# A two-layer encoder step on one core: the first feature pair of SwiGLU in plain products for all chunks, cC's down product in one pass over eight banks, norm sums in two rows

## Chip, cores and metric

The kernel runs on one core of one Trainium2 chip. The metric is the device time of one execution in microseconds. In the kernel before, every product on TensorE (PE) is of 128x128 weights with 128x384 activations in fp32r.

## What is computed

Two encoder layers over a prompt of 1024 frames and eight samples of 16 frames. The part that the change touches is the same in both layers:

```python
def _rms(x, g):
    y = x * lax.rsqrt(jnp.mean(x * x, axis=-1, keepdims=True) + EPS)
    return y * g

def _swiglu(a, w_gate, w_up, w_down):
    return (jax.nn.silu(a @ w_gate) * (a @ w_up)) @ w_down

for i in range(2):                      # layers; D_MODEL = 1024, D_FF = 2816
    a = _rms(h, norm_mix_pre[i])
    mix = ...                           # attention and its out-projection
    h = h + _rms(mix, norm_mix_post[i])
    f = _swiglu(_rms(h, norm_ffn_pre[i]), ffn_w_gate[i], ffn_w_up[i], ffn_w_down[i])
    h = h + _rms(f, norm_ffn_post[i])
    gate = jax.nn.sigmoid(_rms(h, ple_norm[i]) @ ple_w_gate[i] + ple_b_gate[i])
    h = h + gate * (p[i] @ ple_w_proj[i])
```

## The kernel before

The 1024 + 128 frames are 1152 columns, in three **chunks** of 384. `layer_tail` (from L1066) does everything of a layer behind the attention; its argument `order` names the chunks cC, cA, cB in the order in which the out-projection finishes them. Features lie along the partitions, so a 1024-wide vector of a chunk is eight rows of 128x384.

**Products.** fp32 accuracy is had from two fp32r parts: an operand is rounded (a cast on ACT, `round_r`, L139) and the rest is kept as its low part (a subtraction on DVE, `low_part`, L145). `mm3` (L215 to L217) then makes three matmuls for one product: high by high, weight high by activation low, weight low by activation high. Products gather in two kinds of PSUM banks: six in pool `psmm` (tag "mm") and two in `psst` (tag "st"); the norms use the latter.

**SwiGLU.** The 22 blocks of 128 hidden features are taken as 11 **pairs** g, each with a gate and an up **matrix** (g, up) of two blocks A and B. Chunk cC gets plain products (`plain`, 24 matmuls for a block). Chunks cA and cB go together through a form of Strassen with seven products instead of eight (`product`, 12 matmuls each, banks X, Y, Z): weights A, B and their combinations C, D (sums on DVE by `s_sum`, L1315), by activations Y11, Y21 (the halves of cA), Y22 (a half of cB) and T1 to T4, differences of rows of cA and cB (`minus`, L1229). `operand` splits each into parts. A bank is copied out (`copied`, ACT at L1353 or DVE at L1355), added to (`added`, L1359) and finished by silu or by the product with silu (`final`, `direct`); `diff` makes combinations of the results, and `store` sends rows to DRAM: `hc_d` for cC (22 rows), `t_d` for the seven combinations of cA and cB.

Pair 0 (`EARLY`) is split in time: cC's products of both matrices come first, and the seven products of each after them, in the order

```python
product("X", "A", 0, "Y11", new=True)
product("Z", "A", 1, "Y21", new=True, frees=[wa])
product("X", "C", 1, "T2")
product("Y", "D", 0, "T3", new=True)
product("X", "C", 0, "T1", frees=[wc])
product("X", "D", 1, "Y22", frees=[wd])
product("Y", "B", 1, "T4", frees=[wb])
```

**Down product.** `kstep` (from L1513) loads one row of hidden features, splits it, splits one 128x512 half of a block of `w_down`, and makes four output blocks' products (12 matmuls). cC takes two passes of 22 such steps over four "mm" banks, one for each half of the outputs, so each row of `hc_d` is loaded and split twice. The weights are loaded in halves of 256 KB (`wd_load`, L1506). Seven Strassen passes of 11 steps for cA and cB follow.

**Norms.** `plan_rms` squares a chunk on ACT (L360, four squares of 128x768). The first goes into `acc` (one buffer), DVE adds the other three to it (L365) and folds its two rows (L367); PE sums over the partitions (`total`, tile pstat, L233), DVE takes the root in twelve small operations (L241 to L247), PE spreads it over the partitions (`spread`, tile prms, L254) and ACT copies it to `rr` (L380). After the out-projection each chunk has two norms: one of the output, followed by scaling and the residual sum (L424, L428), and one ahead of SwiGLU, followed by scaling (L1195). After the down product there are two again.

**What sets the order.** `Plan` is a list scheduler that runs when the program is built: every step has an engine, a cost in microseconds, steps it comes after, due times and counts of buffers that it takes and frees. It writes out the order of PE, ACT and DVE; SP issues all DMAs in the plan's order too. At run time each engine follows its order and waits on semaphores.

Of the kernel before, what the change touches and what calls it, by code (L numbers as in the profile page):

```python
# [10 lines left out]
F32 = mybir.dt.float32  # L11
F32R = mybir.dt.float32r
# [6 lines left out]
P = 128  # L19
D = 1024  # L20
KT = 8
# [67 lines left out]
def tile_kernel(ctx: ExitStack, tc: tile.TileContext, i, o, upto=99):  # L89
# [260 lines left out]
    def plan_rms(plan, src, after, out="rr", slot=None, ready=()):  # L350
# [4 lines left out]
        def square(k):  # L355
            if k:
                box[k] = t = tp.tile([P, 2, C], F32, name="sq", tag="sq", bufs=NSQ)
            else:
                box["acc"] = t = tp.tile([P, 2, C], F32, name="acc", tag="acc", bufs=1)
            nc.scalar.activation(t, src()[:, 2 * k:2 * k + 2, :], AF.Square)  # L360

        def gather(k):
            acc = box["acc"]
            if k < 4:
                nc.vector.tensor_tensor(acc, acc, box.pop(k), ADD)  # L365
            else:
                nc.vector.tensor_tensor(acc[:, 0], acc[:, 0], acc[:, 1], ADD)  # L367

        def sums():
            box["ps"] = total(box["acc"][:, 0])  # L370
# [11 lines left out]
        last = begin = plan.add(ACT, 0.735, step(square, 0), after[0], takes=["acc"])  # L382
        for k in range(1, 4):
            box["read"] = s = plan.add(ACT, 0.735, step(square, k), after[k] + [begin], takes=["sq"])
            last = plan.add(DVE, 0.87, step(gather, k), [s, last], frees=["sq"])
        last = plan.add(DVE, 0.47, step(gather, 4), [last])
# [679 lines left out]
    def layer_tail(l, oc, Wo, oa0, order, specs_kv=(), more=None):  # L1066
# [18 lines left out]
        plan = Plan(act=4 + (len(oa0[1]) == KT), raw=1, w0=2, w1=3, acc=1, sq=NSQ, rr=NRR, st=2, mm=6, hs=STB, row=NROW, y=2)  # L1085
# [163 lines left out]
        operand("Y21", cA, 4)  # L1249
        operand("Y22", cB, 4)  # L1250
# [39 lines left out]
        def matrix(g, up, when=1):  # L1290
# [58 lines left out]
            def copied(n, bank, eng=ACT):  # L1349

                def fn():
                    if eng == ACT:
                        nc.scalar.copy(put_row(temp(n)), ps(bank))  # L1353
                    else:
                        nc.vector.tensor_copy(put_row(temp(n)), ps(bank))  # L1355
                add(eng, 0.37 if eng == ACT else 0.47, fn, r=[(m, "ps", bank)], w=[(g, temp(n))], takes=["row"], **soon())
# [31 lines left out]
            whole = ("A", x1, [(m, "x", 0)]), ("B", x2, [(m, "x", 1)])  # L1388
            early = m in EARLY
            if when == 0:  # L1390

                loads()
                tags[m] = [parts_of(m, *x) for x in whole]
                unload()
# [4 lines left out]
            loads()  # L1399
            wa = tags[m][0] if early else parts_of(m, *whole[0])  # L1400
            add(DVE, 0.6, step(s_sum, 1), r=[(m, "x", 1)], w=[(m, "s1")], takes=["y"])
            add(DVE, 0.6, step(s_sum, 2), r=[(m, "x", 0), (m, "s1")], w=[(m, "s2")])
            wc = parts_of(m, "C", lambda: sums[m][:, 0], [(m, "s1"), (m, "s2")])
            add(DVE, 0.6, step(s_sum, 3), r=[(m, "x", 0), (m, "x", 1), (m, "s1")], w=[(m, "s3")])
            add(DVE, 0.6, step(s_sum, 4), r=[(m, "x", 0), (m, "s2")], w=[(m, "s4")])
            wd = parts_of(m, "D", lambda: sums[m][:, 1], [(m, "s3"), (m, "s4")])
            release(["y"], [(m, f"s{n}") for n in range(1, 5)])
            wb = tags[m][1] if early else parts_of(m, *whole[1])
            unload()

            product("X", "A", 0, "Y11", new=True)
            copied("11", "X")
            if not early:
                plain(0, "A", [])
                plain_out(0)
            product("Z", "A", 1, "Y21", new=True, frees=[wa])
            added("11", "Z", ["mm"])
            final("11")
            product("X", "C", 1, "T2")
            copied("21", "X", DVE if up else ACT)  # L1420
            product("Y", "D", 0, "T3", new=True)
            product("X", "C", 0, "T1", frees=[wc])
            copied("22", "X")
            added("22", "Y", [])
            final("22")
            if not early:
                plain(1, "B", [])
                plain_out(1)
            product("X", "D", 1, "Y22", frees=[wd])
            direct("r12", lambda: ps("X"), (m, "ps", "X"))  # L1430
            product("Y", "B", 1, "T4", frees=[wb])
            added("21", "Y", ["mm"])
            final("21")
            marks.append(plan.tiles[-1])
            if up:
# [12 lines left out]
        tags = {}  # L1448
        EARLY = (0, 0), (0, 1)
        for m in EARLY:  # L1450
            matrix(*m, when=0)
        for g in range(FFT // 2):
            for up in range(2):
                matrix(g, up)
# [48 lines left out]
        def wd_load(f, half):  # L1503
            if half == 0 and f % 3 == 0:
                wds[f // 3] = ap_.tile([P, 3, 1024], F32, name="wd", tag="act")
# [741 lines left out]
```

## Time and profile before

| | us |
|---|---|
| median of 3 runs (lowest to highest) | 2988.94 (2987.65 to 2989.17) |
| the profiled execution's own time | 2988.7 |
| its span in the profile | 2986.9 |

The span is what the profile covers; times in its rows count from its start. Layer 0's out-projection ends at 715.6 us, its down product begins at 1277.8; in layer 1 it is 2054.8 and 2605.9. A row of the timeline has the start, the length, engine, line, operation, written and read tiles with their shapes, and in brackets how long the engine was idle before it and who released it. A row of a stage table has the stage, its length, the busy time of PE, of its weight loads, of DVE, ACT and POOL (with counts), PE's granted clock as a share of full speed, the busy share of the DMA engines and GB/s.

### The profile page before, as it was taken

To read this page: it belongs to the slowest core of one execution; us is meant where nothing else is said; L and a number is where in the kernel's file an instruction comes from. 1 tells how busy PE (TensorE), PEld (TensorE's weight loads), DVE (VectorE), ACT (ScalarE), POOL (GpSimd) and SP (SyncE) were. 2 spreads that over 40 slices of the span, in tenths; PEclk is the share of its full clock that TensorE was granted. 3 is DMA by queue.
4 is the path that set the end of the run, shared out by engine and by line. 5 is a ranking of instruction groups with operands and counts; after the bars stand their busy time and mean duration, and the time that the engine had idled before them with its cause. 6 is when DMAs were issued, how large, how long until landed. Compare 5 with 4: busy or idle time off the path is not lost. (4 is left out here: it accounts for less than half of the span.)

```text
span 2986.9 us, 48188 instructions
## 1 busy us (share of the span) xinstructions
PE 2873.0 (96%) x17564; PEld 2753.4 (92%) x17564; DVE 1894.1 (63%) x4187; ACT 1279.5 (43%) x2652; POOL 198.0 (7%) x324
## 2 busy tenths in 40 slices
PE   8999999998799999999999999998799999999999
PEld 8999877798699999999999988898799999999999
DVE  6253477767766656558878436658755555459875
ACT  6222266654433333345544245744433333255542
POOL 0000155400000000000000022200000000000000
PEclk9999999999799999999999999999899999999999
DMA  7364577534144444563365667344233333553364
GB/s 257 106 201 144 166 191 196 135 121 130 68 154 153 156 160 161 174 216 93 113 211 191 204 201 225 113 142 130 75 122 115 112 116 114 174 163 105 102 210 147
DMA packets 307041, 453.15 MB, mean 152 GB/s; under 512 B 40002, under 2 KB 253380, under 8 KB 306772
## 3 DMA queue, kind: packets, MB, share of 16 engines
q1 hardware_dynamic: 306804, 450.08, 47.9%
q8 instruction: 138, 2.26, 0.3%
q14 instruction: 99, 0.81, 0.1%
HBM read 315.60 MB, written 136.20 MB: 151 GB/s over the span
## 5 line engine op out<-in xcount | busy, mean ns | idle before, releaser
L215 PE MATMUL ps<-ahi,whi 128*128 128x384 f32 x1008 | 343.6, 341 | 0.7 <-ACT ev L589 0.7
L217 PE MATMUL ps<-ahi,wlo 128*128 128x384 f32 x1008 | 340.1, 337 | 0.2 <-DMA wlo<-wpg_d 0.2
L216 PE MATMUL ps<-alo,whi 128*128 128x384 f32 x1008 | 339.9, 337 | 0.0
L215 PE MATMUL pd<-row,whi 128*128 128x384 f32 x968 | 330.5, 341 | 9.5 <-ACT row L139 9.5
L216 PE MATMUL pd<-row,whi 128*128 128x384 f32 x968 | 329.8, 341 | 0.7 <-DVE row L145 0.7
L217 PE MATMUL pd<-row,wlo 128*128 128x384 f32 x968 | 328.5, 339 | 0.0
L215 PE MATMUL ps<-chi,whi 128*128 128x384 f32 x704 | 235.5, 335 | 0.0
L217 PE MATMUL ps<-chi,wlo 128*128 128x384 f32 x704 | 235.2, 334 | 0.0
L216 PE MATMUL ps<-clo,whi 128*128 128x384 f32 x704 | 235.2, 334 | 0.0
L145 DVE TENSOR_TENSOR wlo<-wraw,whi 128x1024 fp32r<-128x1024 f32 (+3 forms) x146 | 171.6, 1178 | 88.5 <-ACT whi L139 88.1
L139 ACT CAST whi<-wraw 128x1024 fp32r<-128x1024 f32 (+3 forms) x146 | 148.5, 1017 | 160.6 <-PE pX L216 58.3
L139 ACT CAST whi<-wd 128x512 fp32r<-128x512 f32 x198 | 122.4, 620 | 188.8 <-PE pd L216 165.6
L215 PEld LDWEIGHTS ps<-ahi,whi 128*128 128x128 f32 x1008 | 191.8, 190 | 6.2 <-issue 4.9
L145 DVE TENSOR_TENSOR wlo<-wd,whi 128x512 fp32r<-128x512 f32 x198 | 135.8, 688 | 95.2 <-ACT whi L139 93.5
L215 PEld LDWEIGHTS pd<-row,whi 128*128 128x128 f32 x968 | 183.3, 189 | 11.9 <-ACT row L139 10.8
L217 PEld LDWEIGHTS ps<-ahi,wlo 128*128 128x128 f32 x1008 | 191.4, 190 | 0.7 <-DMA wlo<-wpg_d 0.5
L216 PEld LDWEIGHTS ps<-alo,whi 128*128 128x128 f32 x1008 | 191.7, 190 | 0.0
L216 PEld LDWEIGHTS pd<-row,whi 128*128 128x128 f32 x968 | 183.2, 189 | 1.8 <-DVE row L145 1.8
L217 PEld LDWEIGHTS pd<-row,wlo 128*128 128x128 f32 x968 | 183.0, 189 | 0.0
L215 PE MATMUL pX<-T,whi 128*128 128x384 f32 x352 | 120.6, 342 | 37.6 <-ACT whi L139 28.7
L139 ACT CAST whi<-y 128x1024 fp32r<-128x1024 f32 x88 | 92.7, 1053 | 124.4 <-DVE y L1315 62.7
L1353 ACT COPY row<-pX 128x384 f32<-128x384 f32 x110 | 52.5, 477 | 218.0 <-PE pX L217 216.7
(273 smaller groups left out, 7244.2 us busy)
## 6 DMA issues: line engine op xcount, KB each, us to landing
t_d<-row SPq DMA_DIRECT2D x154, 192.0 KB
row<-t_d SPq DMA_DIRECT2D x154, 192.0 KB
wraw<-in_w_gate SPq DMA_DIRECT2D x48, 512.0 KB
wraw<-in_w_up SPq DMA_DIRECT2D x48, 512.0 KB
wd<-in_w_down SPq DMA_DIRECT2D x88, 256.0 KB
row<-hc_d SPq DMA_DIRECT2D x88, 192.0 KB
wpg_d<-sq SPq DMA_DIRECT2D x64, 256.0 KB
st<-h_d SPq DMA_DIRECT2D x72, 192.0 KB
```

The lines of the kernel that those rows point to most:

```text
L139: return nc.scalar.copy(out, in_)
L145: return nc.vector.tensor_tensor(out, x, hi.bitcast(F32), SUB)
L215: nc.tensor.matmul(ps, w[0], a[0], start=first, stop=False, skip_group_check=more)
L216: nc.tensor.matmul(ps, w[0], a[1], start=False, stop=False, skip_group_check=more)
L217: nc.tensor.matmul(ps, w[1], a[0], start=False, stop=last, skip_group_check=more)
L1353: nc.scalar.copy(put_row(temp(n)), ps(bank))
```

## The change

Five things are changed, in both layers.

- **Pair 0 in plain form for all chunks.** `matrix(g, up, 0)` loads and splits A and B and returns a function `on(c)`; for cA (Y11, Y21) and for cB (Y12, a new operand, and Y22) it makes plain products through `halves` (12 matmuls for half a block's sum, 48 for a chunk and matrix). So pair 0 takes 144 matmuls per matrix instead of 132, in the order cC, cA, cB, each for gate and up. T1 to T4 are first read by matrix (1,0).
- **Product order.** In all other matrices X·C·T2 stands ahead of Z·A·Y21, and the copy of X behind it is always ACT's.
- **cC's down product in one pass** of 22 steps of 24 matmuls over six "mm" and two "st" banks; the first step begins with the two "st" banks. `wd_load` fetches a block's 512 KB at once, and each row of `hc_d` is loaded once.
- **Norm sums.** All four squares go to tiles "sq"; DVE adds their eight rows one after the other into an `acc` of 128x384, of which there are now two.
- **Costs.** The costs that the plan reckons with go with these.

```diff
@@ plan_rms
         def square(k):
-            if k:
-                box[k] = t = tp.tile([P, 2, C], F32, name="sq", tag="sq", bufs=NSQ)
-            else:
-                box["acc"] = t = tp.tile([P, 2, C], F32, name="acc", tag="acc", bufs=1)
+            box[k] = t = tp.tile([P, 2, C], F32, name="sq", tag="sq", bufs=NSQ)
             nc.scalar.activation(t, src()[:, 2 * k:2 * k + 2, :], AF.Square)
-        def gather(k):
-            acc = box["acc"]
-            if k < 4:
-                nc.vector.tensor_tensor(acc, acc, box.pop(k), ADD)
-            else:
-                nc.vector.tensor_tensor(acc[:, 0], acc[:, 0], acc[:, 1], ADD)
+        def gather(k, half):
+            t = box[k]
+            if k == 0:
+                box["acc"] = acc = tp.tile([P, C], F32, name="acc", tag="acc", bufs=2)
+                nc.vector.tensor_tensor(acc, t[:, 0], t[:, 1], ADD)
+            else:
+                nc.vector.tensor_tensor(box["acc"], box["acc"], t[:, half], ADD)
...
@@ layer_tail
         operand("Y21", cA, 4)
+        operand("Y12", cB, 0)
         operand("Y22", cB, 4)
...
-            def copied(n, bank, eng=ACT):
...
+            def copied(n, bank):
+                add(ACT, 0.37, lambda: nc.scalar.copy(put_row(temp(n)), ps(bank)), r=[(m, "ps", bank)], w=[(g, temp(n))], takes=["row"], **soon())
...
             if when == 0:
                 loads()
-                tags[m] = [parts_of(m, *x) for x in whole]
+                tags = [parts_of(m, *x) for x in whole]
                 unload()
-                for j in range(2):
-                    plain(j, "AB"[j], [])
-                    plain_out(j)
-                return
+                def halves(j, n, names):
+                    def mms(p):
+                        if p == 0:
+                            tiles[m, n] = psmm.tile([P, 512], F32, name="ps", tag="mm")
+                        hi, lo = units_[m, "AB"[j]]
+                        a_ = acts[names[p]]
+                        for q in range(4):
+                            ws = slice((4 * p + q) * P, (4 * p + q + 1) * P)
+                            mm3(tiles[m, n][:, :C], (hi[:, ws], lo[:, ws]), (a_[:, q], a_[:, 4 + q]), p == q == 0, p == 1 and q == 3)
...
+                    direct(n, lambda: tiles[m, n][:, :C], (m, "ps", n))
+                def on(c):
+                    for j in range(2):
+                        if c == cC:
+                            plain(j, "AB"[j], [])
+                            plain_out(j)
+                        else:
+                            halves(j, f"r{j + 1}{1 + (c == cB)}", ("Y11", "Y21") if c == cA else ("Y12", "Y22"))
...
+                return on
...
+            product("X", "C", 1, "T2")
+            copied("21", "X")
             product("Z", "A", 1, "Y21", new=True, frees=[wa])
             added("11", "Z", ["mm"])
             final("11")
-            product("X", "C", 1, "T2")
-            copied("21", "X", DVE if up else ACT)
             product("Y", "D", 0, "T3", new=True)
...
+        first = [matrix(0, up, 0) for up in range(2)]
+        for c in order:
+            for on in first:
+                on(c)
+        for g in range(1, FFT // 2):
             for up in range(2):
                 matrix(g, up)
...
-            nc.sync.dma_start(wd(f, half), i["w_down"][l, f][:, half * 512:(half + 1) * 512])
+            nc.sync.dma_start(wds[f // 3][:, f % 3], i["w_down"][l, f])
...
-        for half in range(2):
-            dpass([(step(wd, f, half), ("W", f, half), hc_d[f], ("hc", f)) for f in range(FFT)], True,
-                  y_copy(cC, 4 * half, True, half == 0))
+        for f in range(FFT):
+            kstep(lambda f=f: wds[f // 3][:, f % 3], [("W", f, 0), ("W", f, 1)], hc_d[f], ("hc", f), True, f == 0, f == FFT - 1,
+                  y_copy(cC, 0, True, True), 8)
```

**PE at the start of layer 0's SwiGLU.** Before, behind the last of cC's plain products for pair 0 (ps from chi and clo, cC's parts); Y_8476 is Y11:

```order
L217 MATMUL ps<-chi,wlo 128x384
L233 MATMUL pstat<-ones,acc 128x1 x3
L254 MATMUL prms<-ident,ry 128x128 x3
L233 MATMUL pstat<-ones,acc 128x1 x3
L254 MATMUL prms<-ident,ry 128x128 x3
L215 MATMUL pX<-Y_8476,whi 128x384
L216 MATMUL pX<-Y_8476,whi 128x384
L217 MATMUL pX<-Y_8476,wlo 128x384
```

Four groups of norm sums follow one another there with no product between them. After, the same kind of groups stands among cC's products; this is the place 24 matmuls behind cC's first:

```order
L215 MATMUL ps<-chi,whi 128x384
L216 MATMUL ps<-clo,whi 128x384
L217 MATMUL ps<-chi,wlo 128x384
L254 MATMUL prms<-ident,ry 128x128 x3
L233 MATMUL pstat<-ones,acc 128x1 x3
L215 MATMUL ps<-chi,whi 128x384
L216 MATMUL ps<-clo,whi 128x384
L217 MATMUL ps<-chi,wlo 128x384
```

A prms and a pstat group (of cA's and of cB's norms) have moved up to a quarter of cC's products, which go on behind them. And where pair 0 ends and the first product with a T operand begins (Y_8720 is Y22, T_8807 is T2):

```order
L215 MATMUL ps<-Y_8720,whi 128x384
L216 MATMUL ps<-Y_8720,whi 128x384
L217 MATMUL ps<-Y_8720,wlo 128x384
L215 MATMUL pX<-T_8807,whi 128x384
L216 MATMUL pX<-T_8807,whi 128x384
L217 MATMUL pX<-T_8807,wlo 128x384
```

Between the two pieces stand the rest of cC's products, cA's, X·A·Y11 and a plain block of cC of matrix (1,0), and cB's.

**DVE ahead of the low parts of the first C and D.** Before (T_8592, T_8580, T_8544 and T_8613 are T2, T3, T1 and T4; L1229 makes the differences, L1315 the sums for C and D, and wlo from y is a low part of C or D):

```order
L145 TENSOR_TENSOR T_8592<-y,T_8592 128x384 x4
L145 TENSOR_TENSOR T_8580<-y,T_8580 128x384 x4
L145 TENSOR_TENSOR T_8544<-y,T_8544 128x384 x4
L1229 TENSOR_TENSOR y<-y 128x384 x4
L145 TENSOR_TENSOR T_8613<-y,T_8613 128x384 x2
L1315 TENSOR_TENSOR y<-wraw 128x512
L145 TENSOR_TENSOR T_8613<-y,T_8613 128x384
L1315 TENSOR_TENSOR y<-y,wraw 128x512
L1315 TENSOR_TENSOR y<-wraw 128x512
L1315 TENSOR_TENSOR y<-wraw,y 128x512
L145 TENSOR_TENSOR T_8613<-y,T_8613 128x384
L145 TENSOR_TENSOR wlo<-y,whi 128x1024 x2
```

After, behind the lows of T2, T3 and T1 (T_8896 is T4; L1228 is the old L1229, L1369 and L1381 make products and differences of result rows of pair 0):

```order
L1228 TENSOR_TENSOR y<-y 128x384 x2
L1369 TENSOR_TENSOR row<-row,ps 128x384
L1228 TENSOR_TENSOR y<-y 128x384
L1381 TENSOR_TENSOR row<-row 128x384
L1228 TENSOR_TENSOR y<-y 128x384
L1315 TENSOR_TENSOR y<-wraw 128x512
L145 TENSOR_TENSOR T_8896<-y,T_8896 128x384
L1315 TENSOR_TENSOR y<-y,wraw 128x512
L1315 TENSOR_TENSOR y<-wraw 128x512
L1315 TENSOR_TENSOR y<-wraw,y 128x512
L1369 TENSOR_TENSOR row<-row,ps 128x384
L145 TENSOR_TENSOR wlo<-y,whi 128x1024
```

The low of C has the operations on pair 0's result rows (L1369, L1381) ahead of it, and T4's lows have moved partly behind it.

**ACT at the start of layer 0's down product.** Before (whi from wd is a cast of weights of the down product, row from row that of a row of hidden features; L1371 and L1364 are silu, L1353 a copy of bank X):

```order
L1371 ACTIVATE row<-pX 128x384
L1364 ACTIVATE row<-row 128x384
L1353 COPY row<-pX 128x384
L139 CAST whi<-wd 128x512 x3
L1353 COPY row<-pX 128x384
L139 CAST whi<-wd 128x512 x3
L139 CAST row<-row 128x384 x2
L139 CAST whi<-wd 128x512 x2
L139 CAST row<-row 128x384 x3
L139 CAST whi<-wd 128x512
L139 CAST row<-row 128x384
```

After (L1366, L1359 and L1351 are those lines):

```order
L1366 ACTIVATE row<-pX 128x384
L1359 ACTIVATE row<-row 128x384
L1351 COPY row<-pX 128x384
L139 CAST whi<-wd 128x1024 x2
L1351 COPY row<-pX 128x384
L139 CAST whi<-wd 128x1024
L1351 COPY row<-pX 128x384
L139 CAST whi<-wd 128x1024 x3
L139 CAST row<-row 128x384 x3
L139 CAST whi<-wd 128x1024
L139 CAST row<-row 128x384 x2
L139 CAST whi<-wd 128x1024
```

The casts of weights are 1024 wide instead of 512; six of them stand ahead of the first cast of a row in both.

More of the change, by code (lines that the diff above doesn't have):

```diff
@@ L380, in copy @@
             nc.scalar.copy(r, box["pr"][:, :C])
[L382 to L386, printed above, removed]
+        s = last = None
+        for k in range(4):
+            box["read"] = s = plan.add(ACT, 0.735, step(square, k), after[k] + [s], takes=["sq"] if k else ["sq", "acc"])
+            if k:
+                last = plan.add(DVE, 0.47, step(gather, k, 0), [s, last])
+            last = plan.add(DVE, 0.47, step(gather, k, 1), [s, last], frees=["sq"])
         last = plan.add(PE, 0.65, sums, [last], takes=["st"], frees=["acc"], first=True)
@@ L1386, in diff, with combined @@
                 add(DVE, 0.47, lambda: nc.vector.tensor_tensor(R(out_), R(x), R(y_), SUB), r=[(g, x), (g, y_)], w=[(g, out_)], **soon(3.0))
[L1388 to L1392, printed above, removed]
-                tags[m] = [parts_of(m, *x) for x in whole]
-                unload()
-                for j in range(2):
-                    plain(j, "AB"[j], [])
-                    plain_out(j)
-                return
[L1399 to L1418, printed above, removed]
-            product("X", "C", 1, "T2")
-            copied("21", "X", DVE if up else ACT)
[L1421 to L1435, printed above, removed]
+            def combined():
                 diff("u11", "r12", "r11")
@@ new lines, in matrix @@
+            loads()
+            wa = parts_of(m, *whole[0])
+            add(DVE, 0.6, step(s_sum, 1), r=[(m, "x", 1)], w=[(m, "s1")], takes=["y"])
+            add(DVE, 0.6, step(s_sum, 2), r=[(m, "x", 0), (m, "s1")], w=[(m, "s2")])
+            wc = parts_of(m, "C", lambda: sums[m][:, 0], [(m, "s1"), (m, "s2")])
+            add(DVE, 0.6, step(s_sum, 3), r=[(m, "x", 0), (m, "x", 1), (m, "s1")], w=[(m, "s3")])
+            add(DVE, 0.6, step(s_sum, 4), r=[(m, "x", 0), (m, "s2")], w=[(m, "s4")])
@@ new lines, in matrix @@
+            wd = parts_of(m, "D", lambda: sums[m][:, 1], [(m, "s3"), (m, "s4")])
+            release(["y"], [(m, f"s{n}") for n in range(1, 5)])
+            wb = parts_of(m, *whole[1])
+            unload()
+            product("X", "A", 0, "Y11", new=True)
+            copied("11", "X")
+            plain(0, "A", [])
+            plain_out(0)
+            product("X", "C", 1, "T2")
+            copied("21", "X")
+            product("Z", "A", 1, "Y21", new=True, frees=[wa])
+            added("11", "Z", ["mm"])
@@ new lines, in matrix @@
+            final("11")
+            product("Y", "D", 0, "T3", new=True)
+            product("X", "C", 0, "T1", frees=[wc])
+            copied("22", "X")
+            added("22", "Y", [])
+            final("22")
+            plain(1, "B", [])
+            plain_out(1)
+            product("X", "D", 1, "Y22", frees=[wd])
+            direct("r12", lambda: ps("X"), (m, "ps", "X"))
+            product("Y", "B", 1, "T4", frees=[wb])
+            added("21", "Y", ["mm"])
+            final("21")
```

72 lines of the change are left out of this document (40 added, 32 removed).

## The prediction

> **What bounds the kernel now.** I read the page's busy times first, then its 40 slices, then two tables: time by stage, and who waited for whom.
>
> ```profile
> span 2986.9 us, 48188 instructions
> PE 2873.0 (96%) x17564; PEld 2753.4 (92%) x17564; DVE 1894.1 (63%) x4187; ACT 1279.5 (43%) x2652; POOL 198.0 (7%) x324
> PE   8999999998799999999999999998799999999999
> 700.00:715.50 15.50, 15.50 (x91) 15.50 (x90) 11.19 (x17) 5.37 (x8) 0.00 (x0) 1.00 0.85 274
> 715.50:807.10 91.60, 60.56 (x305) 57.98 (x304) 74.45 (x155) 38.42 (x62) 0.00 (x0) 0.78 0.23 76
> 2054.80:2145.80 91.00, 60.02 (x306) 57.55 (x305) 75.06 (x156) 38.33 (x62) 0.00 (x0) 0.79 0.23 76
> 841.00:1270.00 429.00, 420.54 (x2413) 417.99 (x2413) 257.80 (x449) 145.02 (x249) 0.00 (x0) 1.00 0.50 161
> ```
>
> PE is the bound: 2873.0 of 2986.9 us busy, so at most 114 us of waiting can go, plus whatever a low granted clock costs. The slices show PE below 9 tenths at two places only, around 750 and 2100 us. The stage rows (length, then busy PE, PEld, DVE, ACT, POOL, granted clock, DMA) name them: both are the start of a layer's SwiGLU, where PE is busy 60.6 of 91.6 us at a clock of .78. The out-projection before it ran without a gap. In the matrices after it PE is short by only 8.5 us in 429. What PE waits for at the start of layer 0's SwiGLU:
>
> ```profile
> PE pX L215 <- ACT whi L139: 14.3, 1, 14.3
> PE prms L254 <- DVE ry L247: 5.6, 2, 3.0
> PE pZ L216 <- DVE Y L145: 5.0, 1, 5.0
> PE pstat L233 <- DVE acc L367: 4.9, 2, 4.0
> ```
>
> These 30 us are one cause: PE has done cC's plain products and has nothing left that doesn't hang on the norms of cA and cB, done one after the other on DVE.
>
> **Start of SwiGLU, the main term.** The length of one matmul's slot, and the ends of the stage:
>
> ```profile
> 711.93 0.33 PE L215 MATMUL ps<-ohi,whi 128*128 128x384 f32 x1
> 715.57 0.33 PE L215 MATMUL ps<-chi,whi 128*128 128x384 f32 x1
> 734.29 0.80 PE L233 MATMUL pstat<-ones,acc 128*128 128x1 f32 x6 [0.89 <-DVE acc L367]
> 774.88 0.69 PE L215 MATMUL pX<-T,whi 128*128 128x384 f32 x1 [14.33 <-ACT whi L139]
> 807.12 0.33 PE L215 MATMUL pX<-Y,whi 128*128 128x384 f32 x1
> ```
>
> From 711.93 to 715.57 lie 21 matmuls: .1733 us each. From cC's first matmul (715.57) to the first product of matrix (1,0) (807.12) are 91.55 us. In them stand 276 matmuls: for each matrix of pair 0 cC's 48 and seven products of 12, and a piece of 12 of (1,0)'s cC that is drawn forward. To the same state of the work the changed kernel needs 2 x 144 + 12 = 300, or 52.0 us: the plain form costs 24 matmuls (4.2 us) more per layer. Six small groups of sums stand between: from 715.57 to PE's stop at 733.40 (734.29 less .89) are 17.83 us for 96 matmuls (16.64) and two groups, less the last matmul's tail of .16: 1.0 a pair, 3.0 in all.
>
> What is left is the waiting S after the change. I walk the new rows (as the order in the section on the change has them) with these durations: the twelve small operations of a root 2.4 with what follows them, and from runs of n the step, T's lows (5.70 - .07)/12 = .47 and scalings .53. All 128x384 operations of two tensors on DVE get .47, a group of sums .6, a copy of rr with its hand-over .7.
>
> ```profile
> 720.49 0.16 DVE L241 TENSOR_SCALAR rv<-pstat 128x3 f32<-128x3 f32 x1 [1.78 <-PE pstat L233]
> 722.66 0.16 DVE L247 SCALAR_TENSOR_TENSOR ry<-rt,ry 128x3 f32<-128x3 f32 x1
> 749.42 2.73 DVE L1195 SCALAR_TENSOR_TENSOR y<-y,gains,rr 128x384 f32<-128x384 f32 x5
> 763.57 5.70 DVE L145 TENSOR_TENSOR T<-y,T 128x384 fp32r<-128x384 f32 x12
> 773.08 0.67 DVE L1315 TENSOR_TENSOR y<-y,wraw 128x512 f32<-128x512 f32 x1
> 773.79 1.04 ACT L139 CAST whi<-y 128x1024 fp32r<-128x1024 f32 x1 [2.10 <-DVE y L1315]
> 775.36 2.34 DVE L145 TENSOR_TENSOR wlo<-y,whi 128x1024 fp32r<-128x1024 f32 x2
> ```
>
> cA's second norm now comes ahead of cB's first. PE waits .8 for its sums; the root is done at 719.6, but the group prms stands 24 matmuls on, so rr is there at 722. On DVE follow one scaling, cB's root (2.4), seven scalings, some rows of cB's residual and the lows of Y11 (by 730) and Y21 (by 734.4). PE ends cC's 96 matmuls at 735 and finds both: no wait. cB's residual, its seven adds and two product rows take DVE until 744.9 + .5; PE comes to cB's second group of sums after 60 of cA's 96 matmuls, at 745.4: .5 of waiting. Root, prms and copy end at 751.5; eight scalings, one difference and eight lows (8.5) make Y12 ready at 757.6 and Y22 at some 759.5. PE has cA's rest, X of Y11 (12) and cC's plain part of (1,0) (24) to do until 759.4: no wait, by 1.8 us for Y12 and by as much for Y22, which is wanted 12 matmuls later. cB's 96 end at 776.0, and the next row is X with C and T2.
>
> On DVE stand, behind Y22's last low, 30 operations of .47 (differences, T's lows, product rows), one more T low, four of .6 for C and D, one more product row and C's low of 1.2: 14.1 + .5 + 2.4 + .5 + 1.2 = 18.7, so 778.1. C's cast on ACT ends at 776.4. PE waits .4 for the cast and, two matmuls later, 1.4 for the low: 1.8. Behind PE's row stand only products with C and D, and what the other engines do there waits for these anyway. S = .8 + .5 + 1.8 = 3.1, and I add 1 for slots and banks that a walk misses: 4.1. Its bounds are 1 (the first wait alone) and 14.3 (the wait on the same product now). The stage is then 52.0 + 3.0 + 4.1 = 59.1: **32.4 us less** in layer 0, and, from the 91.0 of the stage row, 31.9 in layer 1; 64.3 together. POOL has nothing there, and the DMA share is .23, so SP's loads, which (1,0) now wants earlier, have room.
>
> A short wait may also cost clock. The first two rows stand behind the 14.33 us of idle above, with 18 matmuls from one to the other: .32 each. The last two are of the norm behind the down product:
>
> ```profile
> 777.10 0.52 PE L215 MATMUL pX<-T,whi 128*128 128x384 f32 x1
> 782.84 0.34 PE L215 MATMUL pY<-T,whi 128*128 128x384 f32 x1
> PE pstat L233 <- DVE acc L367: 2.6, 1, 2.6
> 1568.00:1575.00 7.00, 6.92 (x24) 6.95 (x25) 5.10 (x18) 4.17 (x6) 0.00 (x0) 0.52 0.19 60
> ```
>
> 2.6 us of idle, and the next 7 us ran at .52: some 2.5 us lost beside the wait. At T2 the idle is in two pieces, neither over 1.5, with matmuls between, so I take nothing, and 2.5 per layer stays in the range. The Trainium skill ("TensorE: Matmul & The Clock Gate", Part 1, HAM oscillation) has it that idle gaps over about 3.4 us drop the clock, and that one busy window of about 3.4 us restores it; by that T2's wait would be free as well, and a drop would cost about 1.7 us. The trace disagrees on the threshold, as 2.6 us sufficed, and on the length, 7 us: the measurement decides.
>
> **X's second product in the up matrices.**
>
> ```profile
> PE pX L215 <- DVE row L1355: 8.8, 8, 1.8
> 876.57 1.22 DVE L145 TENSOR_TENSOR wlo<-y,whi 128x1024 fp32r<-128x1024 f32 x1
> 883.09 0.33 PE L215 MATMUL pX<-T,whi 128*128 128x384 f32 x1
> 883.11 1.05 ACT L139 CAST whi<-y 128x1024 fp32r<-128x1024 f32 x1 [0.99 <-PE pZ L216]
> 886.30 1.22 DVE L145 TENSOR_TENSOR wlo<-y,whi 128x1024 fp32r<-128x1024 f32 x1
> 887.43 0.55 DVE L1355 COPY row<-pX 128x384 f32<-128x384 f32 x1
> ```
>
> In layer 0 PE waits 8.8 us for DVE's copy of X, which stands behind a 1.2 us low (886.30, then 887.43). After, the copy is ACT's, and X·C·T2 stands ahead of Z·A·Y21, so two products (Z and Y, 24 x .1733 = 4.2 us) cover it. ACT may have a 1.05 us cast in front, still inside 4.2. I take **-8**; bounds 0 and -8.8. Layer 1 has none to lose.
>
> **Start of the down product.**
>
> ```profile
> PE pd L215 <- ACT row L139: 4.4, 2, 3.5
> PE pd L216 <- DVE row L145: 0.3, 1, 0.3
> 1277.50:1281.00 3.50, 3.23 (x9) 2.92 (x10) 1.05 (x2) 0.72 (x2) 0.00 (x0) 0.53 1.04 388
> 1277.21 1.01 ACT L139 CAST row<-row 128x384 fp32r<-128x384 f32 x2 [2.36 <-DMA hc_d<-row]
> PE pd L215 <- ACT row L139: 5.1, 2, 4.1
> 2605.50:2612.00 6.50, 6.14 (x18) 5.83 (x19) 2.30 (x4) 1.44 (x3) 0.00 (x0) 0.50 0.86 310
> ```
>
> Layer 0 loses 4.4 + .3 of waiting, and 3.2 us of matmuls at .53 cost 1.5: 6.2. Layer 1 loses 5.1 + .3 and half of 6.1: 8.5. The first row comes late by DMA (share 1.04: the transfers are at their limit here), and the second step waits again, since a step lasts 12 matmuls. After, a step lasts 24 (4.2 us) and needs 512 KB of weights and one row of 192 KB, 170 GB/s against the 388 moved here; before it was 256 KB and a row in 2.1 us, 215. The first row's cast now stands behind a 1024-wide cast (1.05) that waits for the last product's weights, and its low behind a 1.2 low: from the last matmul's end .25 + 1.05 + .47 to the high, and 2.9 to the low. I take 3.2 of waiting and no slow clock: -3.0 and -5.3, **about -8**. Bounds -15 (nothing is lost) and -2 (the wait and, in both layers, the slow stretch of layer 1: 2 x 6.3 of 14.7).
>
> **Norm sums in two rows.** DVE adds per norm are 7 x .47 = 3.3 instead of 3 x .87 + .47 = 3.1, but with two accumulators the next norm's squares no longer wait for the last one's sums. Beside the start of SwiGLU this touches the norms behind the down product, with 2.6 us of waiting (row above) and in layer 1
>
> ```profile
> PE pstat L233 <- DVE acc L367: 4.8, 2, 3.4
> ```
>
> cA's sums now stand earlier and gain, cB's stand where they did: **-1**; bounds -4 (half of the 7.4) and +4 (one more norm late, with its clock). Start, attention and end: within .5.
>
> **The sum.** 64.3 + 8 + 8 + 1 = 81.3. The profiled execution took 2988.7 us, .24 below the median of the runs, so nothing is to be corrected: 2988.7 - 81.3 = **2907 us**.
>
> **Rivals.**
> (a) DVE becomes the bound of the start. It has 74.45 us busy in 91.6; ahead of C's low come Y12's four lows and eight row operations, 12 x .47 = 5.6 us. My walk puts them into DVE's idle spots, with 1.8 us to spare at Y12. If they aren't covered, C's low comes at 776.6 + 5.6 = 782.2 instead of 778.1, and the clock drops behind it (2.5): (4.1 + 2.5) x 2 = 13 us: 2920. The same price holds if Y11 or Y12 is late. Chance .2.
> (b) The cover is complete: S = 1, and the down product starts without a stall (-15): 3.1 x 2 + 7 = 13 us less: 2894. For it: the walk's waits are small differences of long sums. Against: C's low has no slack at all. Chance .12.
> (c) Slower: T2 now needs C 2.08 us (12 matmuls) earlier in each of 40 later matrices, and A is freed 2.08 later, for whose slot a cast waits (883.11, for pZ). If C is late each matrix waits; from 81/40 = 2.0 us per matrix the gain is gone, and at 2.5 it is 3007. Against: C's low ended at 877.8 (876.57 + 1.22), 5.3 us ahead of T2 at 883.09. Chance .04.
> (d) The fill does not happen: cA's operands come no earlier than now, and the gap stays. Then only 8 + 8 + 1 less 8.3 for the added matmuls is won: 2980. Against: cA's second norm needs only the out-projection's outputs and free accumulators, which it now has. Chance .05.
>
> **The range.** Forecast .55, (a) .2, (b) .12, (c) .04, (d) .05, another wait of some 10 to 20 us, of which no row warns, .04. From (b) less a few us to (a) plus the open 2.5 per layer, the down product's and the norms' upper bounds: 2888 to 2933. A measurement of this kernel tells .2% (6 us) from no change. Slower by more: .04; within: .02; faster: .94.
>
> **What would show it.** In the profile after: no wait over 3 us between the end of the out-projection and the first T2 product, which should start some 60 us behind cC's first matmul (then -32 is right); a wait there on C's cast or low of 1 to 3 us; no PE wait on a copy of X in the matrices; one wait of 2 to 4 us at the first pd. I am wrong if waits for a product with T2 recur in every matrix, if prms or pstat still wait 3 us each at the start, or if the granted clock there stays near .8.

## The result and the profile after

| | us |
|---|---|
| before, median of 4 runs (lowest to highest) | 2989.06 (2987.65 to 2990.6) |
| after, median of 4 runs | 2902.55 (2900.84 to 2905.61) |
| ratio, 95% interval | .9712 (.9695 to .9728) |
| after, the profiled execution; its span | 2905.61; 2903.8 |

The change makes the kernel 2.9% faster; 2907 was forecast. The page of after, first its busy times and PE's slices:

```profile
span 2903.8 us, 47806 instructions
PE 2855.9 (98%) x17612; PEld 2742.0 (94%) x17612; DVE 1843.5 (63%) x4139; ACT 1259.0 (43%) x2574; POOL 198.0 (7%) x324
PE   8999999999999999999999999999999999999999
```

The two holes around 750 and 2100 us are gone. PE is busy for 17.1 us less although it has 48 matmuls more: most of the slow clock behind the holes went with them. The stages by the same table (length, busy PE, PEld, DVE, ACT, POOL, granted clock, DMA share, GB/s): layer 0's out-projection, the start of its SwiGLU, its matrices, and layer 1's out-projection:

```profile
613.40:723.10 109.70, 106.41 (x605) 105.68 (x603) 70.72 (x147) 51.56 (x86) 0.00 (x0) 0.97 0.40 129
723.10:790.00 66.90, 63.59 (x364) 62.56 (x365) 60.48 (x143) 29.91 (x54) 0.00 (x0) 0.97 0.26 86
840.00:1230.00 390.00, 390.00 (x2252) 390.00 (x2251) 240.52 (x412) 143.65 (x242) 0.00 (x0) 1.00 0.50 162
1910.80:2017.70 106.90, 105.01 (x604) 104.27 (x603) 71.11 (x147) 50.84 (x83) 0.00 (x0) 0.98 0.43 138
```

The start of SwiGLU runs at a clock of .97 instead of .78, and the matrices have no idle time left. But both out-projections, which had run without a gap, now have one. The same two stages before:

```profile
612.10:715.50 103.40, 103.30 (x607) 102.83 (x604) 67.44 (x129) 48.57 (x81) 0.00 (x0) 1.00 0.43 139
1951.80:2054.80 103.00, 103.00 (x604) 102.88 (x604) 67.03 (x129) 47.92 (x79) 0.00 (x0) 1.00 0.45 144
```

What PE waits for in after, over the whole span (waited for, us in total, times, longest):

```profile
PE pstat L233 <- DVE acc L365: 12.4, 8, 3.3
PE ps L215 <- ACT phl L139: 8.6, 2, 8.1
PE pd L216 <- DVE row L145: 2.9, 2, 1.5
PE pd L215 <- ACT row L139: 2.8, 2, 1.4
PE pX L217 <- DVE wlo L145: 2.2, 2, 1.1
PE pX L215 <- ACT whi L139: 2.2, 2, 1.1
```

In before the same view began with 28.7 us for whi, 14.3 a time, and had 17.0 for the norm sums (acc), 11.1 for ry and 8.8 for the copies of X on DVE. Of whi 2.2 are left, ry and the copies are gone, and the norm sums are now the largest. The wait for phl, in the attention, was 8.7 in before.

**Stage by stage.** A stage is measured on PE from its first work to the first of the next, less the wait ahead of it. The ends of both SwiGLUs, before:

```profile
1277.77 0.69 PE L215 MATMUL pd<-row,whi 128*128 128x384 f32 x1 [3.45 <-ACT row L139]
...
2054.83 0.33 PE L215 MATMUL ps<-chi,whi 128*128 128x384 f32 x1
...
2605.86 0.69 PE L215 MATMUL pd<-row,whi 128*128 128x384 f32 x1 [4.07 <-ACT row L139]
```

and after, where a group of norm sums stands first:

```profile
723.79 0.80 PE L233 MATMUL pstat<-ones,acc 128*128 128x1 f32 x6 [0.71 <-DVE acc L365]
...
1240.82 0.45 PE L215 MATMUL pd<-row,whi 128*128 128x384 f32 x1 [1.42 <-ACT row L139]
...
1242.71 0.44 PE L216 MATMUL pd<-row,whi 128*128 128x384 f32 x1 [1.45 <-DVE row L145]
...
2018.20 0.80 PE L233 MATMUL pstat<-ones,acc 128*128 128x1 f32 x6 [0.51 <-DVE acc L365]
...
2534.00 0.45 PE L215 MATMUL pd<-row,whi 128*128 128x384 f32 x1 [1.42 <-ACT row L139]
```

SwiGLU in layer 0 took 1277.77 - 3.45 - 715.57 = 558.8 us before and 1240.82 - 1.42 - 723.08 = 516.3 after (723.08 is 723.79 less its wait of .71), in layer 1 547.0 and 514.9 by the same subtraction. The out-projections grew by 6.3 and 3.9 us. From the down product's start to the layer's end (in layer 0 up to the next out-projection, so with layer 1's attention) it is 6.1 less in layer 0 and 13.9 less in layer 1. Ahead of layer 0's out-projection it is 1.2 more, which is within the scatter: in the traces of the experiments that stretch takes 609.2 to 614.8 us. The sum is -42.4 - 32.1 + 10.2 - 20.0 + 1.2 = -83.1, the difference of the spans.

### The profile page after: what moved, and what is told of

The parts are those of the page before. It is cut to its first block, busy times and chain, and to the rows that moved or that the text cites. A ratio compares the mean times of both kernels' runs of the same rounds, so it can differ in the third digit from the quotient of the medians.

```text
span 2903.8 us, 47806 instructions
## 1 busy us (share of the span) xinstructions
PE 2855.9 (98%) x17612; PEld 2742.0 (94%) x17612; DVE 1843.5 (63%) x4139; ACT 1259.0 (43%) x2574; POOL 198.0 (7%) x324
## 5 line engine op out<-in xcount | busy, mean ns | idle before, releaser
L215 PE MATMUL pd<-row,whi 128*128 128x384 f32 x968 | 325.8, 337 | 3.1 <-ACT row L139 2.8
L216 PE MATMUL pd<-row,whi 128*128 128x384 f32 x968 | 324.5, 335 | 3.0 <-DVE row L145 2.9
L139 ACT CAST whi<-wd 128x512 fp32r<-128x512 f32 (+1 forms) x154 | 114.6, 744 | 160.0 <-PE pd L216 137.2
L145 DVE TENSOR_TENSOR wlo<-wd,whi 128x512 fp32r<-128x512 f32 (+1 forms) x154 | 129.0, 839 | 86.3 <-ACT whi L139 86.3
L1351 ACT COPY row<-pX 128x384 f32<-128x384 f32 x120 | 57.5, 479 | 241.0 <-PE pX L217 236.5
L2019 POOL TENSOR_SCALAR tt<-tt,l 128x256 f32<-128x256 f32 (+1 forms) x128 | 59.7, 484 | 1237.5 <-DMA r<-r_d 1094.7
L215 PEld LDWEIGHTS ps<-chi,whi 128*128 128x128 f32 x704 | 132.2, 188 | 0.0
```

Of the source, the lines that this page charges most:

```text
L139: return nc.scalar.copy(out, in_)
L145: return nc.vector.tensor_tensor(out, x, hi.bitcast(F32), SUB)
L215: nc.tensor.matmul(ps, w[0], a[0], start=first, stop=False, skip_group_check=more)
L216: nc.tensor.matmul(ps, w[0], a[1], start=False, stop=False, skip_group_check=more)
L1351: add(ACT, 0.37, lambda: nc.scalar.copy(put_row(temp(n)), ps(bank)), r=[(m, "ps", bank)], w=[(g, temp(n))], takes=["row"], **soon())
L2019: nc.gpsimd.tensor_scalar(tt[:, g, :nw], tt[:, g, :nw], l[:, g:g + 1], 1.0, op0=MULT, op1=MULT)
```

## The experiments

Unless told otherwise each is an edit of after. The kernel before was run beside each group; ratios are to it, with 95% intervals. Its median lay between 2987.65 and 2989.55 us in the groups. Kernels of different groups ran on different chips, so where ratios overlap, the trace of the edited place decides.

**Pair 0 as before, the rest of the change kept.** The Strassen form of pair 0 returns, in the new order of products; a first tile of tag "row" keeps the row tiles where after has them (why that matters is told below).

```diff
-                tags = [parts_of(m, *x) for x in whole]
+                tags[m] = [parts_of(m, *x) for x in whole]
                 unload()
-                def halves(j, n, names):
...
-                return on
+                for j in range(2):
+                    plain(j, "AB"[j], [])
+                    plain_out(j)
+                return
...
-        for c in order:
-            for on in first:
-                on(c)
-        for g in range(1, FFT // 2):
+        for g in range(FFT // 2):
```

> The changed kernel with pair 0 as before (cC's plain products first, then seven products per matrix), row tiles kept at offset 64. Theory F (the plain form is what fills the gap): 276 matmuls and some 30 us of waiting per layer again, less what the earlier norms of cA save: 2903 + 45 to 64, 2948 to 2967. Rival N (earlier norms fill it as well): T2 is the next thing wanted and waits for cB's norms, but the waits before it go: 2903 + 20 to 30.

Measured 2966.13 us (2958.83 to 2968.57, 4 runs), ratio .9928 (.9911 to .9944): 63.6 more than after. The profiled execution is the fastest of the four; in its trace the two SwiGLUs are 26.5 and 29.0 us longer than in after. Its start of layer 0's SwiGLU, the stage table and what PE waits for there:

```profile
720.00:800.00 80.00, 47.18 (x258) 45.27 (x257) 66.27 (x147) 33.17 (x56) 0.00 (x0) 0.79 0.26 85
```

```profile
PE pX L215 <- ACT whi L139: 23.6, 1, 23.6
PE pstat L233 <- DVE acc L365: 4.3, 1, 4.3
PE prms L254 <- DVE ry L247: 3.6, 2, 2.5
```

So the hole and its slow clock belong to pair 0's Strassen form, and the other edits do not close them. With the new norms it is only gathered in one wait of 23.6 us; the new norms alone, further down, gather it in the same way, in one of 24.3.

**cC's down product in two passes.**

```diff
-        for f in range(FFT):
-            kstep(lambda f=f: wds[f // 3][:, f % 3], [("W", f, 0), ("W", f, 1)], hc_d[f], ("hc", f), True, f == 0, f == FFT - 1,
-                  y_copy(cC, 0, True, True), 8)
+        for half in range(2):
+            dpass([(step(wd, f, half), ("W", f, half), hc_d[f], ("hc", f)) for f in range(FFT)], True,
+                  y_copy(cC, 4 * half, True, half == 0))
```

> The changed kernel with cC's down product in two passes over four banks, rows of hidden features loaded twice; the row tiles stay at offset 64. Theory D (the one pass saves the late second step and the slow clock at the start, and nothing else): the starts cost 6.2 and 8.5 us again instead of 2.9 each, 2903 + 9 = 2912. Rival (the start's waits came from the state in which SwiGLU leaves the queues, which the other edits changed too): within 3 us of 2903.

2912.73 us (2907.8 to 2917.15, 4 runs), ratio .9746 (.9729 to .9762): 10.2 more. PE's waits at the start of layer 0's down product:

```profile
PE pd L215 <- ACT row L139: 5.2, 2, 4.2
PE pd L216 <- DVE row L145: 0.3, 1, 0.3
```

The stall of before (4.4 and .3) is back where after waits 1.42 + 1.45. In the trace, that of the fastest of the four runs, the stages from the down product on are 1.9 and 4.0 us longer than in after, so 5.9 of the 10.2 are seen there.

**The old order of X and Z, and the up matrices' copy of X on DVE.**

```diff
-            product("X", "C", 1, "T2")
-            copied("21", "X")
             product("Z", "A", 1, "Y21", new=True, frees=[wa])
             added("11", "Z", ["mm"])
             final("11")
+            product("X", "C", 1, "T2")
+            copied("21", "X", DVE if up else ACT)
```

> The changed kernel with Z·A·Y21 ahead of X·C·T2 again and the up matrices' copy of X on DVE. Theory X (the waits of pX for DVE's copy were a cost of their own): they come back in layer 0, 8 to 9 us in all, but the first T2 product, 12 matmuls later, no longer waits for C (2.2 us and some slow clock per layer): 2903 + 9 - 4 = 2908. Rival (the waits hung on the phase of DVE's queue in layer 0, which the new start shifts): no such waits, 2899.

2908.23 us (2904.69 to 2910.46, 4 runs), ratio .973 (.9716 to .9745): 5.7 more, with ranges that just overlap. The waits for the copies in layer 0's matrices (840 to 1230 us) are back:

```profile
PE pX L215 <- DVE row L1355: 4.6, 3, 2.1
PE pX L215 <- ACT row L1353: 0.8, 2, 0.5
```

Against that, T2's wait in matrix (1,0) falls from 2.2 to .4 us per layer, since C has 12 matmuls more time. So the new order saves waits of 5.4 us in layer 0's later matrices and costs some 1.8 at the first matrix of each layer.

**The old norm sums.**

```diff
-        def gather(k, half):
...
+        def gather(k):
+            acc = box["acc"]
+            if k < 4:
+                nc.vector.tensor_tensor(acc, acc, box.pop(k), ADD)
...
-        plan = Plan(act=4 + (len(oa0[1]) == KT), raw=1, w0=2, w1=3, acc=2, sq=NSQ, rr=NRR, st=2, mm=6, hs=STB, row=NROW, y=2)
+        plan = Plan(act=4 + (len(oa0[1]) == KT), raw=1, w0=2, w1=3, acc=1, sq=NSQ, rr=NRR, st=2, mm=6, hs=STB, row=NROW, y=2)
```

> The changed kernel with the norm sums of the kernel before (acc of two rows, one buffer, three wide adds and a fold). Theory N (the two accumulators let cA's second norm run ahead of cB's first, and this carries a large part of the gain at the start of SwiGLU; the same edit makes the new wait of 3.3 us at a norm inside layer 0's out-projection and 1.9 in layer 1): the out-projection is 10 us shorter in both layers together, but PE waits at cA's and cB's norms some 5 us or more per layer, 2900 to 2915. Rival F (the plain form alone fills the gap, the norms only follow): the start is as in the changed kernel, the out-projection's 10 us come back, 2893.

2909.04 us (2907.98 to 2909.18, 4 runs), ratio .9737 (.9723 to .975): 6.5 more. The out-projections run without a gap again, in 103.0 and 103.1 us, so it is the new norm that made them longer. But SwiGLU pays for it: it is 3.9 and 6.2 us longer than in after, 10.1 together, against 10.5 won in the out-projections. The 3.3 us by which the two traces differ come from the other stages, above all from layer 1's last one, 7.7 longer, where PE waits 4.1 us for norm sums instead of 2.0. PE's waits at the start of layer 0's SwiGLU (780 to 800 us):

```profile
PE pX L215 <- ACT whi L139: 5.5, 1, 5.5
PE pX L217 <- DVE wlo L145: 0.7, 1, 0.7
```

The wait does not come at the groups of sums, as my theory had it, but at C, whose sums and cast stand behind the norms on DVE and ACT.

**The new norm sums alone, on the kernel before.** The hunk of `plan_rms` in the change, and `acc=2`.

> The kernel before with nothing but the new norm sums (seven narrow adds, two accumulators). Theory F (without plain products to fill it, the gap at the start of SwiGLU ends when cB's operands and C are ready, so earlier norms of cA bring little): start of SwiGLU shorter by 0 to 4 us per layer, the out-projections longer by 6 and 4 us through the new wait: 2985 to 2998. Rival N (the two accumulators are what shortens the chain of norms): start shorter by 8 to 15 us per layer, 2969 to 2983.

2987.05 us (2983.05 to 2992.88, 10 runs), ratio .9998 (.9989 to 1.0007). The out-projections are 8.1 and 5.5 us longer, the SwiGLUs 8.8 and 6.2 shorter: alone, the norms only move the wait. The time is as theory F had it, but the start of SwiGLU gains some 6 to 7 us per layer, more than its 0 to 4 and less than the rival's 8 to 15. The norms pay with the plain pair, which uses the earlier cA and cB.

**Why the down product's matmuls got faster.** Some 30 to 70 us into the down product, where PE waits for nothing, the same matmuls took less time in after than before. Two rows of before, then of after, 60 matmuls apart:

```profile
1310.46 0.34 PE L215 MATMUL pd<-row,whi 128*128 128x384 f32 x1
...
1321.02 0.34 PE L215 MATMUL pd<-row,whi 128*128 128x384 f32 x1
```

```profile
1310.30 0.33 PE L215 MATMUL pd<-row,whi 128*128 128x384 f32 x1
...
1320.70 0.33 PE L215 MATMUL pd<-row,whi 128*128 128x384 f32 x1
```

.1760 and .1733 us each, at a granted clock of 1.00 in both. Over all slots of the down products without wait and slow clock the means are .1759 and .1735, so the 2904 matmuls give 2904 x .0024 = 7 us, of which the prediction knows nothing. The difference that I found in the matmuls themselves is where their moving operand lies: three steps without cost (`put_row` for u11, u22, u21) let the plan take the row tiles first of all tiles, and they begin at byte 170048 of a partition instead of 213440. Three kernels ask whether it is the change's order of work (O), the place (P) or the offset within a few hundred bytes (A). In the kernel before, a row tile taken first:

```diff
+        row()
+
         def tile_steps(key, unit, act, needs_w, needs_a, frees=(), pieces=2):
```

> The kernel before, with one row tile taken first, so that the ten row tiles lie at bytes 170048 to 185408 of a partition instead of 213440 to 228800; nothing else moves in the order. Theory P (the place of the row tiles sets the spacing of the down product's matmuls): spacing .1733 us instead of .1755 to .1760, 2904 matmuls x .0024 = 7 us less, about 2982. Theory A (their offset modulo 512 does, 64 here instead of 448): the same here. Theory O (the spacing comes from less work on ACT and DVE beside the pass): spacing stays near .176, time 2989.

2981.28 us (2977.41 to 2984.55, 11 runs), ratio .9976 (.9967 to .9985), 6.5 less than before, with one line that computes nothing. Its rows:

```profile
1310.52 0.33 PE L215 MATMUL pd<-row,whi 128*128 128x384 f32 x1
...
1320.92 0.33 PE L215 MATMUL pd<-row,whi 128*128 128x384 f32 x1
```

.1733: O falls. In after, the row tiles put back high, at byte 213056:

```diff
+        for n_, sh, k_ in (("st", [P, C], STB), ("sq", [P, 2, C], NSQ), ("acc", [P, C], 2), ("y", [P, KT, C], 2), ("rr", [P, C], NRR)):
+            tp.tile(sh, F32, name=n_, tag=n_, bufs=k_)
```

> The changed kernel, with the other tiles taken first, so that the row tiles lie at the end of the partition (from byte 213056, offset 64 modulo 512 as in the changed kernel). Theory P: spacing in the down product back at .1755 to .1760, 7 us more, about 2910. Theory A: spacing .1733, 2903. Theory O: .1733, 2903.

2901.16 us (2899.33 to 2905.68, 5 runs), ratio .9711 (.9698 to .9724); the same spacing, .1733: P falls. In after, low, but 384 bytes on:

```diff
+        tp.tile([P, 96], F32, name="pad", tag="pad", bufs=1)
+        row()
```

> The changed kernel with 384 bytes left free ahead of the row tiles: they start at byte 170432, offset 448 modulo 512 as in the kernel before. Theory P and O: spacing .1733, about 2903. Theory A: .176, about 2910.

2905.03 us in one run. Its rows:

```profile
1318.03 0.34 PE L215 MATMUL pd<-row,whi 128*128 128x384 f32 x1
...
1328.59 0.34 PE L215 MATMUL pd<-row,whi 128*128 128x384 f32 x1
```

.1760, and from the first matmul of a down product (with its wait) to the last it is 3.5 and 3.6 us longer than with the tiles high: A holds. The one time says less, as it lies within the range of the previous kernel's runs and 5 us under the forecast. An offset of 64 bytes past a multiple of 512 (170048, 213056) gave .1733, one of 448 (213440, 170432) gave .1760. To find the rule, row tiles 1568 bytes apart, so that their offsets run from 64 to 352 by 32:

```diff
-            return tp.tile([P, C], dt, name="row", tag="row", bufs=NROW)
+            return tp.tile([P, C + 8], dt, name="row", tag="row", bufs=NROW)[:, :C]
```

> The changed kernel with the ten row tiles 1568 bytes apart instead of 1536, so that their offsets modulo 512 are 64, 96, 128 and so on to 352. Theory A256 (the offset modulo 256 decides: 64 fast, 192 slow): fast at 64 and 320, slow somewhere between, slowest about 192. Theory A512 (only offsets near 448 are slow): all ten at .1733. Matmuls are told apart by the tile that they read; the time lies between 2900 and 2910.

2912.57 us in one run, above the forecast range. In layer 0's pass of cC the first two full steps ran at .1735, the later ones at .1746 to .1757 in the mean, above .1733 and below .1760. Both rules that I had put forward miss; which offsets cost what is still open.

**The first matrix in the old order.** What the kernel with the old order showed, used: Z·A·Y21 first in (1,0) only.

```diff
+            if m == (1, 0):
+                product("Z", "A", 1, "Y21", new=True, frees=[wa])
+                added("11", "Z", ["mm"])
+                final("11")
+                product("X", "C", 1, "T2")
+                copied("21", "X")
+            else:
...
```

> The changed kernel with Z·A·Y21 ahead of X·C·T2 in matrix (1,0) alone, where C is late. Theory C (the 2.2 us at the first T2 product per layer are DVE's queue ahead of C's low, and 12 matmuls hide them): no wait at T2 in either layer, 4 to 6 us less, about 2898. Rival (Z's bank or Y21 takes the place, or X's copy comes late behind it): the wait moves on, 2902.

2899.78 us (2898.29 to 2904.45, 4 runs), ratio .9707 (.9692 to .9723). T2's waits fall to .38 us per layer, but 2.8 us less than after, where 4 to 6 were expected, is within what the runs scatter.

**The wait in the out-projection.** In layer 0 of after, PE before cC's second norm:

```profile
674.14 1.41 PE L233 MATMUL pstat<-ones,acc 128*128 128x1 f32 x6 [3.27 <-DVE acc L365]
675.41 0.67 PE L215 MATMUL ps<-ohi,whi 128*128 128x384 f32 x1
675.88 0.52 PE L216 MATMUL ps<-olo,whi 128*128 128x384 f32 x1
...
679.72 0.52 PE L216 MATMUL ps<-olo,whi 128*128 128x384 f32 x1
```

A wait of 3.27 us, then 14 matmuls at .32 instead of .1733. Two causes offered themselves. The sums come some 1.1 us later than before, as DVE's residual sums wait for rows of the old h by DMA, 2.52 us at the first:

```profile
666.20 0.56 DVE L427 TENSOR_TENSOR mix<-mix,st 128x384 f32<-128x384 f32 x1 [2.52 <-DMA st<-in_xT]
...
670.37 0.56 DVE L427 TENSOR_TENSOR mix<-mix,st 128x384 f32<-128x384 f32 x1 [1.14 <-DMA st<-in_xT]
```

And PE's group stands 12 matmuls earlier. It is the second of four groups of sums; they stand after 18, 27, 37 and 48 pieces of 12 matmuls of the out-projection, and in before after 19, 28 and 37, the fourth two pieces into SwiGLU. The norm edit makes the move: alone on the kernel before it puts the group after 27 pieces too, and with the old sums it is after 28 again; that this comes of the narrower last adds in the plan's costs is my reading. In before PE came to the group just on time:

```profile
671.80 0.80 PE L233 MATMUL pstat<-ones,acc 128*128 128x1 f32 x6
```

First, with Z first in (1,0), the stores of the new h, which share SP's queue with those rows, four rows at a time:

```diff
-            if k % 2:
-                nc.sync.dma_start(fm(h_d, c)[:, k - 1:k + 1, :], mix[c][:, k - 1:k + 1, :])
+            if k % 4 == 3:
+                nc.sync.dma_start(fm(h_d, c)[:, k - 3:k + 1, :], mix[c][:, k - 3:k + 1, :])
```

> As the run before, and cC's residual rows are stored to DRAM four at a time instead of two, so that three loads of residual rows stand ahead of the first store in the DMA queue. Theory S (inside the out-projections the norm of cC is late since loads of residual rows stand behind these stores and the weights' loads): the waits of 3.3 and 1.9 us and the slow clock behind them go, 5 to 10 us less than the run before, about 2890. Rival (the loads are late through the weights' transfers alone): the waits stay, 2898.

2904.46 us (2898.54 to 2907.71, 4 runs), ratio .9724 (.9707 to .9741). DVE's first wait for a row falls to 1.36 us and the second grows to 2.48; PE's waits in the two layers stay at 3.45 and 2.23. The spacing of the stores is not the cause. Then, again with Z first, the order: cC's second group of sums one piece later on PE.

```diff
-        last = plan.add(PE, 0.65, sums, [last], takes=["st"], frees=["acc"], first=True)
+        last = plan.add(PE, 0.65, sums, [last, *late], takes=["st"], frees=["acc"], first=True)
...
+            rms = plan_rms(plan, lambda c=c: mix[c], pairs(res), late=plan.tiles[39:40] if c == cC else ())
```

> As the run with Z·A·Y21 first in matrix (1,0), and PE's group of sums for cC's second norm made to come after one more piece of 12 matmuls of the out-projection, where the kernel before has it (336 matmuls after the out-projection's first, instead of 324). Theory M (the plan, reckoning with the narrower adds, placed this group 12 matmuls, 2.08 us, ahead of what the residual's rows allow): the waits at the second norm fall from 3.4 to 1.3 and from 2.6 to .5 us and the slow clock behind the first goes: 5 to 6 us less, about 2894. Rival (the sums come later by as much, since what is late is DVE's own queue): the waits stay, 2900.

**2891.61 us** (2888.75 to 2893.7, 5 runs), ratio .967 (.9656 to .9683), clear of after's and of the kernel it edits: the fastest of all. What PE waits for in layer 0's out-projection:

```profile
PE pstat L233 <- DVE acc L365: 1.6, 2, 1.3
```

1.29 of it is at cC's second norm, where the kernel that it edits waits 3.38 and after 3.27; in layer 1 that wait is gone. DVE's last adds are not earlier, in after and here:

```profile
672.84 1.15 DVE L365 TENSOR_TENSOR acc<-acc,sq 128x384 f32<-128x384 f32 x2 [0.50 <-ACT sq L357]
...
670.54 1.15 DVE L365 TENSOR_TENSOR acc<-acc,sq 128x384 f32<-128x384 f32 x2 [0.51 <-ACT sq L357]
```

They end 60.6 and 60.7 us after the out-projection's start (613.40 and 611.00), and 59.5 in before. The out-projections take 104.8 and 103.3 us by the measure of the stages, 109.7 and 106.9 in after, 108.4 and 106.1 in the kernel that it edits. Of the 10.2 us that they had grown by 8.6 are back, 6.5 of them against the kernel that it edits: that was the position of the group in PE's order, 12 matmuls or 2.1 us too early. The rest goes with the later sums; whether DMA alone makes them late wasn't settled.

## Why the prediction was right, and where not

The undone parts cost 63.6 (plain pair), 10.2 (one pass), 6.5 (norms), 5.7 (order) and 6.5 (row tiles, by the kernel before): 92.5 together for a gain of 86.5. Each is a difference of medians that scatter by some us, so the 6 us over prove no overlap; the norms do hang on the plain pair, as alone they gain nothing.

| term | forecast | measured |
|---|---|---|
| start of SwiGLU | -64.3 | -65.7 |
| copies of X | -8 | -8.8 |
| down product to the layer's end | -9 | -20.0 |
| out-projections | 0 | +10.2 |
| the rest | 0 | +1.2 |
| sum | -81.3 | -83.1 |

**Start of SwiGLU: right, cause and size.** What the SwiGLUs lost, 42.4 less 8.8 of X's waits, is 33.6 in layer 0, and 32.1 in layer 1, against 32.4 and 31.9. The first T2 product begins 60.6 us behind cC's first matmul (724.45), where some 60 were forecast. The walk gave waits of .8 at cA's group, .5 at cB's and .4 + 1.4 at T2. In the trace they are .71 (723.79), .43, and at T2

```profile
785.02 0.45 PE L215 MATMUL pX<-T,whi 128*128 128x384 f32 x1 [1.09 <-ACT whi L139]
786.75 0.69 PE L217 MATMUL pX<-T,wlo 128*128 128x384 f32 x1 [1.10 <-DVE wlo L145]
787.23 0.52 PE L215 MATMUL pX<-T,whi 128*128 128x384 f32 x1
```

1.09 + 1.10. That is 3.3 us of waiting, and 3.0 in layer 1, where the walk had 3.1 and the sum 4.1. Waits for Y12 and Y22, which the walk ruled out by 1.8 us, do not appear. So rival (a), DVE as the bound, did not come about, nor (d). Rival (b) had the cover complete at T2 and at pd; 2.2 and 2.9 us of waiting stand there. Rival (c), C late in every matrix, is refuted by the stage row: 390.00 of 390.00 us busy. A clock penalty did follow T2's waits in layer 0 (8 matmuls at .32, 1.3 us) and did not in layer 1; the 2.5 us held open for it was too much. The stretch of before that this price was read from lost some 3 us rather than 2.5: 6 sums and 17 matmuls took 6.75 us from 1568.08 on, where 3.7 would do at full clock.

**Copies of X: right.** All 8.8 us went, and putting the old order back returned 5.4 in the same matrices.

**Start of the down product: right in kind.** Waits of 1.42 + 1.45 per layer against 3.2; the slow clock, taken as none, came in layer 0 (10 matmuls at .32, 1.6 us). Of the 14.7 us lost before, 14.7 - 2 x 2.87 - 1.6 = 7.4 are won, of 8 forecast.

**The rest of the down stages: not forecast.** 7 us come from the row tiles' offset. The norms behind the down product are mixed: in layer 1 PE waits 2.0 us for them instead of 4.8, in layer 0 3.3 instead of 2.6, so 2.1 against the 1 forecast. Some 3.5 us of the 20.0 are left; about 2.0 of them are fewer matmuls in slots near .32 behind the down products (46 in after, 60 in before), the rest is not assigned.

**Out-projections: the step that failed.** The prediction says "Start, attention and end: within .5" and counts the norm's effect only at the start of SwiGLU and behind the down product. But the same `plan_rms` makes cC's two norms inside the out-projection, and with the new one PE's group of sums moves ahead by 12 matmuls, past the point at which its operand is there. The order of the changed kernel has that move in it; the prediction reads PE's order only where PE was already waiting. The miss cost 10.2 us, of which the group's old place gives back 6.5 (8.6 with what Z first in (1,0) changed), and was hidden by the row tiles' 7 and by the unassigned rest. That the sum came out within 2 us of the spans' difference is in part luck: errors of opposite sign, beside the main term, which was good.

## What to carry to other kernels

When a shared helper's cost changes, list every place where it is called, also those without a wait today: an engine that works in order and never waits may have been on time by less than one piece of work. And before a gain is credited to an edit of the order, compare the spacing of equal instructions in stretches without waits, since an edit can move buffers to other addresses.

## What the runs showed of the hardware

- **The offset of a moving operand costs matmul time.** With the same 128x384 fp32r matmul and a granted clock of 1.00, .1733 us at an offset of 64 past a multiple of 512 bytes and .1760 at 448, each with the tiles low and with the tiles high in the partition; .1746 to .1757 in most steps with ten offsets mixed. The rule behind it is open.
- **A wait of 1 to 2 us can be followed by half clock, or not.** Layer 1's out-projection in after had a wait of 1.89 us (at 1970.15) and then 9 matmuls at .32, at a granted clock of .50. T2's two waits of 1.1 us were followed by 8 such matmuls in layer 0 and by none in layer 1 (granted clock .50 and 1.00 in the 3 us behind); at pd it was 10 and none, with equal waits in both layers. So the length of the wait alone doesn't decide. The Trainium skill ("TensorE: Matmul & The Clock Gate", Part 1, HAM oscillation) has it that idle gaps over about 3.4 us drop the clock; the trace disagrees, as it did in the prediction, since 1.89 us sufficed.
